# Packing the two score triangles of the C heads into one block, with the spreading on GpSimd

## The chip, the cores and the metric

The kernel runs on one NeuronCore of a Trainium2 chip. The metric is the device time of one execution in microseconds (us), the median of the runs shown. Engines are named as in the profile: PE (TensorE, matmuls; PEld its weight loads), DVE (VectorE), ACT (ScalarE), POOL or GpSimd, and SP, whose queue issues most DMAs. `L739` means line 739 of the kernel before; the changed kernel has line numbers of its own.

## The reference, cut to what matters

One layer of a hybrid decoder over 512 tokens of width 2048: RMS norm, one input projection, three token mixers side by side (A: 8 dilated heads, B: a convolution, C: 16 sliding-window heads), an output projection with residual, then a SwiGLU feed-forward with residual. All in float32. The change touches mixer C alone:

```python
def _band_attention(q, k, v, max_dist, sinks=None):
    """Causal banded attention: query t attends keys t-max_dist .. t."""
    ...
    s = jnp.einsum('nbqhgd,nbkhd->nbhgqk', qb, kb) * (hd ** -0.5)
    ...
    valid = (dist >= 0) & (dist <= max_dist) & (kpos[:, None, :] >= 0)
    s = jnp.where(valid[None, :, None, None], s, -jnp.inf)
    m = jnp.max(s, axis=-1)
    m = jnp.maximum(m, sk)                      # sk: one learned sink per head
    p = jnp.exp(s - m[..., None])
    denom = jnp.sum(p, axis=-1) + jnp.exp(sk - m)
    o = jnp.einsum('nbhgqk,nbkhd->nbqhgd', p, vb) / denom_t[..., None]
...
cq = _rms_norm(cq.reshape(B, S, C_Q_HEADS, HEAD_DIM), c_q_g[l])
ck = _rms_norm(ck.reshape(B, S, C_KV_HEADS, HEAD_DIM), c_k_g[l])
out_c, _ = _band_attention(cq, ck, cv, C_WINDOW - 1, sinks=c_sinks[l])
```

With a window of 128 and blocks of 128 queries, a query block i sees its own key block (there the lower triangle is valid, the diagonal included) and the block before (there the strict upper triangle is valid). The two triangles have no column in common: each query has at most 128 valid keys.

## The kernel before, in words

Activations lie transposed, 128 channels by 512 tokens in a tile. The program has four stages, one behind the other on PE: the input projection, tile by tile (`PROJ`, L315 to L317), the output projection (the same lines, tiles `o`), the gate and up products (L1089) and the down product (L1347 to L1349). Every float32 product is made of three fp32r matmuls: each operand is split into a high part (an ACT cast) and a low part (a DVE subtraction), and high x high, high x low and low x high are summed. The weights are split on the fly: ACT casts the high part (`wh`, L286), DVE subtracts to get the low part (`wl`, L264), two units of weights ahead of PE, with three buffers for each part.

The order is written out by hand. The mixers run in the shadow of the input projection: `project` issues 48 matmuls a tile, and at every second k step it calls `ticks.tick()`, which issues what is due at that tick on all engines (`Ticks.after(n, fn)`). Six projection matmuls lie between two ticks, and each engine runs its instructions in the order of issue. The convolution's taps (L524, L526, on DVE, one every 1.9 ticks) and its gate product (L517, on GpSimd) are placed the same way.

A C projection tile `cq` holds two heads. `head_scales` gets their RMS scales: a square on ACT, a sum on DVE, a DMA out and back, then three small GpSimd instructions (L606 to L608) that write `rq`. `attention` then places two heads, `every` = 6 ticks apart, by `C_TICKS = (ready, every, step, s1, sx, s2, fl, ev, we)`. For one C head, in ticks from its start t0:

| tick | function | what it issues |
|---|---|---|
| 0 and 2 | `scores` u = 0, 1 | PE, L739 and L740: scores of query blocks 0, 1 (u = 0; 128 + 256 keys) and 2, 3 (u = 1; 256 + 256) into a PSUM bank each |
| 2 and 4 | `top` | DVE, L746: adds the mask `bias_c` and takes the row maxima; L749 and L751 turn them into the exponent's bias |
| 4 and 6 | `exps` | ACT, L759 with the row sums; L762 for the sink |
| 6 and 8 | `norm` | DVE, L768, L773, L775: divides by the row sums |
| 13 and 14 | `flip` | PE, L791: transposes of 128x128 blocks, four and then three |
| 14 and 15 | `high` | ACT, L797: high part of the transposed block |
| 15 and 16 | `low` | DVE, L802: low part |
| 19 | `weigh` | PE, L815 and L816: eight matmuls with the values |
| 20 and 21 | `out_high`, `out_rows` | ACT L824 and DVE L829: into the tile `mix_c` |

`UNITS` lists which scores share a bank, `TBANKS` which transposed blocks stand side by side, so that one key block serves two query blocks in one matmul. Tiles of 128x512 come from one pool of `N_SLOTS` = 73 slots; a tile that is written into a slot waits for the last reader of the slot's tile before. PSUM has six banks for the mixers and two for the projection. A heads go through the same functions with `A_TICKS`, behind the C heads.

Of the kernel before, what the change touches and what calls it, by code (L numbers as in the profile page):

```python
# [24 lines left out]
BIG = -1.0e30  # L25
# [13 lines left out]
SD, VD, EV = 7, 4, 1  # L39


C_TICKS = (1, 6, 2, 2, 2, 2, 5, 1, 3)
A_TICKS = (0, 8, 2, 1, 3, 1, 3, 1, 2)


# [36 lines left out]
C_G1, C_G2, C_CW, C_CB, C_LG, C_LB, C_QK, C_SINK, C_ALL = 0, 16, 32, 156, 160, 164, 168, 172, 188  # L82
# [34 lines left out]
def kernel(ctx: ExitStack, tc: tile.TileContext, xT, wi, wo, wgu, wd, cst_in, outT):  # L117
    nc = tc.nc
# [89 lines left out]
    for t, (g, r) in enumerate(DOWN):  # L208
        first, end = RANGES[r]
        base = len(works)  # L210
# [5 lines left out]
        for k in ("21A", "11A", "21B", "11B", "22A", "22B", "12A", "12B"):  # L216
            c = k[2]
# [128 lines left out]
    ident = cp.tile([P, P], F32, name="ident")  # L346
# [4 lines left out]
    def col(i):  # L351
        return cst[:, i:i + 1]
# [17 lines left out]

    mult_a = slot("mult_a")
    bias_a = slot("bias_a")
    bias_c = slot("bias_c", cols=2 * P)
    gqk = cp.tile([P, 2], F32, name="gqk")
    nsink = cp.tile([P, 16], F32, name="nsink")
    di = slot("di", I32)
    nc.gpsimd.iota(di, pattern=[[-1, T]], base=3 * P, channel_multiplier=1)
    di2 = slot("di2", I32)
    nc.gpsimd.iota(di2[:, :2 * P], pattern=[[-1, 2 * P]], base=P, channel_multiplier=1)

    def masks():
        df, m4, r = slot("df"), slot("m4", I32), slot("r")
        nc.vector.tensor_copy(df, di)
        nc.vector.tensor_single_scalar(m4, di, 3, op=ALU.bitwise_and)
        nc.vector.tensor_scalar(r, m4, 0.0, None, op0=ALU.is_equal)
        nc.vector.scalar_tensor_tensor(mult_a, df, 128.0, r, op0=ALU.is_le, op1=ALU.add)
        nc.vector.tensor_single_scalar(m4, di, 15, op=ALU.bitwise_and)
        nc.vector.tensor_scalar(r, m4, 0.0, None, op0=ALU.is_equal)
        nc.vector.tensor_add(mult_a, mult_a, r)
        nc.vector.scalar_tensor_tensor(mult_a, df, 0.0, mult_a, op0=ALU.is_ge, op1=ALU.mult)  # L390
        nc.vector.tensor_scalar(bias_a, mult_a, 0.0, BIG, op0=ALU.is_equal, op1=ALU.mult)
        nc.vector.tensor_copy(df[:, :2 * P], di2[:, :2 * P])
        nc.vector.tensor_scalar(r[:, :2 * P], df[:, :2 * P], 127.0, None, op0=ALU.is_le)
        nc.vector.scalar_tensor_tensor(r[:, :2 * P], df[:, :2 * P], 0.0, r[:, :2 * P], op0=ALU.is_ge, op1=ALU.mult)
        nc.vector.tensor_scalar(bias_c, r[:, :2 * P], 0.0, BIG, op0=ALU.is_equal, op1=ALU.mult)
        for i in range(2):
            nc.vector.scalar_tensor_tensor(gqk[:, i:i + 1], col(C_QK + 2 * i), 8.0, col(C_QK + 2 * i + 1),
                                           op0=ALU.mult, op1=ALU.mult)
        nc.vector.tensor_scalar(nsink, cst[:, C_SINK:C_SINK + 16], -1.0, None, op0=ALU.mult)
# [42 lines left out]
    for k in range(KT):  # L442
# [9 lines left out]
        elif k < 4 or k % 2 == 0:  # L452
            wh, wl = next_unit()
            o = 0
# [9 lines left out]
        hi, lo = h_hl.pop(k)  # L464
# [15 lines left out]
    r1b = slot("r1b")  # L480
# [199 lines left out]
    def do_v(box, b, name):  # L680
# [35 lines left out]
    def attention(kind, box, mix, mi, heads):  # L716
        ready, every, step, s1, sx, s2, fl, ev, we = C_TICKS if kind == "c" else A_TICKS

        if mi in ROWS[-2:]:
            fl, we = fl + 2, we + 3  # L720
        name = mi
        us = UNITS[kind]
        mask = bias_c if kind == "c" else bias_a
        mw = mask.shape[-1]
        st = {}

        def head(h):
# [5 lines left out]
            def scores(u):  # L733
# [3 lines left out]
                for i, k0, n, o in us[u]:  # L737
                    qs, ks = slice(i * P, (i + 1) * P), slice(k0, k0 + n)
                    nc.tensor.matmul(b[:, o:o + n], q[:, qs], kh[:, ks], start=True, stop=False)  # L739
                    nc.tensor.matmul(b[:, o:o + n], q[:, qs], kl[:, ks], start=False, stop=True)  # L740

            def top(u):
                b, rq = banks[u], box["rq"]
                s = slice(us[u][0][0], us[u][-1][0] + 1)
                for i, k0, n, o in reversed(us[u]):
                    nc.vector.tensor_tensor_reduce(b[:, o:o + n], b[:, o:o + n], mask[:, mw - n:],  # L746
                                                   op0=ALU.add, op1=ALU.max, scale=1.0, scalar=-3.0e38,
                                                   accum_out=mx[:, i:i + 1])
                nc.vector.scalar_tensor_tensor(nm[:, s], mx[:, s], -1.0, rq[:, s, h], op0=ALU.mult, op1=ALU.mult)  # L749
                if kind == "c":  # L750
                    nc.vector.tensor_scalar(nm[:, s], nm[:, s], nsink[:, heads[h]:heads[h] + 1], None, op0=ALU.min)  # L751

            def exps(u):
                b, rq = banks.pop(u), box["rq"]
                e = es[u] = slot(f"{name}e{h}{u}")
                s = slice(us[u][0][0], us[u][-1][0] + 1)
                for i, k0, n, o in us[u]:
                    acc = dict(accum_out=den[:, i:i + 1]) if kind == "c" else {}
                    nc.scalar.activation(e[:, o:o + n], b[:, o:o + n], AF.Exp, bias=nm[:, i:i + 1],  # L759
                                         scale=rq[:, i, h:h + 1], **acc)  # L760
                if kind == "c":
                    nc.scalar.activation(mx[:, s], nm[:, s], AF.Exp, bias=col(C_SINK + heads[h]))  # L762

            def norm(u):
                e = es[u]
                s = slice(us[u][0][0], us[u][-1][0] + 1)
                if kind == "c":
                    nc.vector.tensor_add(den[:, s], den[:, s], mx[:, s])  # L768
                else:
                    for i, k0, n, o in us[u]:  # L770
                        nc.vector.scalar_tensor_tensor(e[:, o:o + n], e[:, o:o + n], 1.0, mult_a[:, T - n:],
                                                       op0=ALU.mult, op1=ALU.mult, accum_out=den[:, i:i + 1])
                nc.vector.reciprocal(rd[:, s], den[:, s])  # L773
                for i, k0, n, o in us[u]:
                    nc.vector.tensor_scalar(e[:, o:o + n], e[:, o:o + n], rd[:, i:i + 1], None, op0=ALU.mult)  # L775
# [244 lines left out]
        ticks.tick()  # L1020
    lows_now()
    ticks.drain()
    b = m_hi = m_lo = r1b = mult_a = bias_a = bias_c = None

    lows_now()
    late_lows.clear()
# [467 lines left out]
```

## Time and profile before

| what | value |
|---|---|
| median of 3 runs | 1872.05 us (1872.03 to 1872.28) |
| profiled execution, its own time | 1872.28 us |
| its span, first to last instruction | 1870.5 us |
| PE busy | 1864.2 us (100%) |
| DVE, ACT, POOL busy | 1466.2, 1345.4 and 1072.9 us |
| granted TensorE clock | 1.00 |
| C heads, first scores to last weigh | 99 to 331 us |

The span is what the profile covers; the run's own time holds some 1.8 us more. Busy time is the time in which an engine had an instruction under way; matmuls overlap, so a row's duration on PE is longer than the distance to the next row's start. In rows of a timeline the first number is the start, the second the duration, both in us, and a bracket at the end gives the idle time before it and what ended it.

### The profile page before, as it was taken

The numbers are of one execution on the slowest core, as the hardware profiler recorded it, in microseconds if no ns is written. First come the engines' busy times: TensorE is split into PE (matmuls) and PEld (weight loads), VectorE is DVE, ScalarE is ACT, GpSimd is POOL, SyncE is SP. The second block draws the span as 40 slices with busy tenths as digits, with TensorE's granted clock in tenths as the row PEclk, the third lists the DMA queues.
The fourth block names the chain that finished last, engine by engine and source line by source line (L and its number), as shares of the span: only waits on it lengthen the run. The fifth ranks groups of instructions, "written<-read, shape, count | busy, mean of one in ns | idle before, by whom it ended". The sixth has DMA issues, their size and how long they took to land.

```text
span 1870.5 us, 28387 instructions
## 1 busy us (share of the span) xinstructions
PE 1864.2 (100%) x9654; PEld 1597.0 (85%) x9654; DVE 1466.2 (78%) x2451; ACT 1345.4 (72%) x1872; POOL 1072.9 (57%) x700
## 2 busy tenths in 40 slices
PE   9999999999999999999999999999999999999998
PEld 7888888888888888888888888888888888888887
DVE  6789978998689777777777777777777777777767
ACT  6356654553457888888888888888888877778775
POOL 0111011100003877877878778787787879879775
PEclk9999999999999999999999999999999999999999
DMA  7242243343333445565555645556456967666645
GB/s 272 83 138 80 86 131 101 93 125 135 119 135 112 136 169 159 159 194 155 180 158 157 195 156 180 158 159 194 143 169 238 325 217 239 214 225 230 205 134 113
DMA packets 213329, 307.39 MB, mean 164 GB/s; under 512 B 75200, under 2 KB 124992, under 8 KB 213184
## 3 DMA queue, kind: packets, MB, share of 16 engines
q1 hardware_dynamic: 213040, 305.57, 51.2%
q8 instruction: 76, 1.25, 0.3%
q14 instruction: 69, 0.57, 0.1%
q10 hardware_dynamic: 144, 0.01, 0.0%
HBM read 244.03 MB, written 53.09 MB: 159 GB/s over the span
## 4 chain that ended last, share of the span: by engine, by line
PE 100%; DVE 0%; issue 0%; ACT 0%; DVEq 0%
PE out L1089 46%; PE out L1349 7%; PE out L1348 7%; PE out L1347 7%; PE o L315 3%; PE o L317 3%; PE o L316 3%; PE cq L315 2%; PE cq L317 2%; PE cq L316 2%; PE aq L317 1%; PE aq L315 1%; PE ak L315 1%; PE av L315 1%; PE ak L317 1%; PE av L316 1%
## 5 line engine op out<-in xcount | busy, mean ns | idle before, releaser
L1089 PE MATMUL out<-h,wh 128*128 128x512 f32 x2464 | 588.6, 391 | 0.0
L1089 PEld LDWEIGHTS out<-h,wh 128*128 128x128 f32 x2464 | 452.9, 188 | 87.3
L1089 PEld LDWEIGHTS out<-h,wl 128*128 128x128 f32 x2464 | 315.9, 191 | 12.0
L1089 PE MATMUL out<-h,wl 128*128 128x256 f32 x2464 | 319.7, 283 | 0.0
L1347 PE MATMUL out<-wh,a 128*128 128x512 f32 x620 | 240.6, 388 | 0.0
L1349 PE MATMUL out<-wh,a 128*128 128x512 f32 x620 | 240.5, 388 | 0.0
L1348 PE MATMUL out<-wl,a 128*128 128x512 f32 x620 | 240.5, 388 | 0.0
L286 ACT CAST wh<-w 128x1024 fp32r<-128x1024 f32 (+2 forms) x94 | 96.8, 1031 | 141.7 <-PE o L316 62.6
L264 DVE TENSOR_TENSOR wl<-w,wh 128x1024 fp32r<-128x1024 f32 (+2 forms) x95 | 112.7, 1187 | 31.3 <-ACT wh L286 31.0
L1348 PEld LDWEIGHTS out<-wl,a 128*128 128x128 f32 x620 | 116.4, 188 | 24.0
L1347 PEld LDWEIGHTS out<-wh,a 128*128 128x128 f32 x620 | 116.4, 188 | 23.8
L1349 PEld LDWEIGHTS out<-wh,a 128*128 128x128 f32 x620 | 116.4, 188 | 23.7
L1357 DVE TENSOR_TENSOR y<-y,out 128x512 f32<-128x512 f32 x164 | 106.4, 683 | 26.5 <-PE out L1349 24.9
L526 DVE SCALAR_TENSOR_TENSOR y<-bu,cst,y 128x511 f32<-128x511 f32 (+14 forms) x120 | 87.4, 729 | 0.4
L315 PE MATMUL o<-mh_c,wh 128*128 128x512 f32 x128 | 51.1, 399 | 0.0
L315 PE MATMUL cq<-hh,wh 128*128 128x512 f32 x128 | 51.1, 399 | 0.0
L317 PE MATMUL o<-mh_c,wl 128*128 128x512 f32 x128 | 50.0, 391 | 0.0
L317 PE MATMUL cq<-hh,wl 128*128 128x512 f32 x128 | 50.0, 391 | 0.0
L316 PE MATMUL o<-ml_c,wh 128*128 128x512 f32 x128 | 49.9, 390 | 0.0
L316 PE MATMUL cq<-hl,wh 128*128 128x512 f32 x128 | 49.9, 390 | 0.0
L431 POOL TENSOR_TENSOR lvr<-lvv,nhalf 128x4 f32<-128x4 f32 x1 | 1.9, 1919 | 70.8 <-DVE lvv L430 70.8
L182 POOL TENSOR_TENSOR w('s', 'g0')_5732<-w('21', 'g0')_5578,w('22', 'g0')_5576 128x1024 f32<-128x1024 f32 x1 | 2.5, 2457 | 69.0 <-DVE wl L264 69.0
(2999 smaller groups left out, 4930.9 us busy)
## 6 DMA issues: line engine op xcount, KB each, us to landing
od<-a SPq DMA_DIRECT2D x154, 256.0 KB, 4.7
a<-od SPq DMA_DIRECT2D x154, 256.0 KB, 5.6
w<-in_wi SPq DMA_DIRECT2D x58, 512.0 KB, 3.5
w<-in_wo SPq DMA_DIRECT2D x32, 512.0 KB, 3.5
x<-in_xT SPq DMA_DIRECT2D x16, 256.0 KB, 6.9
xr<-in_xT SPq DMA_DIRECT2D x16, 256.0 KB, 3.7
x2d<-xr SPq DMA_DIRECT2D x16, 256.0 KB, 2.0
z<-x2d SPq DMA_DIRECT2D x64, 64.0 KB, 3.7
```

What stands on the lines that cost most here:

```text
L182: nc.gpsimd.tensor_add(out[:, :n], raws[key[a]][0][:, :n], raws[key[b]][0][:, :n])
L264: fn(*args)
L286: (nc.vector.tensor_copy if u == 0 else nc.scalar.copy)(hi[:, :n], t[:, :n])
L315: nc.tensor.matmul(out, wh, xh, start=start, stop=False)
L316: nc.tensor.matmul(out, wh, xl, start=False, stop=False)
L317: nc.tensor.matmul(out, wl, xh, start=False, stop=stop)
L526: nc.vector.scalar_tensor_tensor(yconv[j][:, i:], hconv[j][:, :T - i], c, yconv[j][:, i:], op0=ALU.mult, op1=ALU.add)
L1089: nc.tensor.matmul(out, lhs[:, s], rhs, start=begin, stop=x is xs[-1] and low == flip[0], skip_group_check=True)
L1347: nc.tensor.matmul(b[:, lo:hi], x[:, high], wh[:, s], start=start, stop=False, skip_group_check=True)
L1348: nc.tensor.matmul(b[:, lo:hi], x[:, high], wl[:, s], start=False, stop=False, skip_group_check=True)
L1349: nc.tensor.matmul(b[:, lo:hi], x[:, low], wh[:, s], start=False, stop=last, skip_group_check=True)
L1357: getattr(eng, op)(t, t, src)
```

## The change

In a C head, `pack` takes the place of `top`. Query block 0 is masked as before (its upper triangle gets -1e30). For blocks 1, 2 and 3 a predicated copy on DVE overwrites the upper triangle of the head's own key block with the upper triangle of the block before, in PSUM, so that one block of 128x128 holds all valid scores, and the row maxima are taken over it. The four packed blocks are exponentiated on ACT in one go at tick 6, normalised on DVE by one broadcast multiply at tick 9 and transposed at tick 14 by four transposes into one bank. ACT makes the high part at tick 15, DVE the low part at tick 16. `spread_out` then writes the tiles that `weigh` reads: eight GpSimd selects (`affine_select`) a head, four on the high and four on the low part, which copy the valid triangle of each block and write zero elsewhere: six of 128x256 and two of 128x128. `weigh` is the same as before, at tick 21. The masks change to match: `bias_c` shrinks to 128 columns and a mask `upper` of 128 columns is added, both in one slot. The A heads' functions lose their branches for C.

```diff
--- before.py
+++ after.py
@@ -39,7 +39,7 @@
 SD, VD, EV = 7, 4, 1
 
 
-C_TICKS = (1, 6, 2, 2, 2, 2, 5, 1, 3)
+C_TICKS = (1, 6, 2, 2, 2, 3, 5, 1, 4)
 A_TICKS = (0, 8, 2, 1, 3, 1, 3, 1, 2)
 
 
@@ -370,13 +370,14 @@
 
-    bias_c = slot("bias_c", cols=2 * P)
+    over = slot("over")
+    bias_c, upper = over[:, :P], over[:, P:2 * P].bitcast(I32)
     di2 = slot("di2", I32)
-    nc.gpsimd.iota(di2[:, :2 * P], pattern=[[-1, 2 * P]], base=P, channel_multiplier=1)
+    nc.gpsimd.iota(di2[:, :P], pattern=[[-1, P]], base=0, channel_multiplier=1)
 
     def masks():
         df, m4, r = slot("df"), slot("m4", I32), slot("r")
@@ -389,10 +390,9 @@
         nc.vector.tensor_add(mult_a, mult_a, r)
         nc.vector.scalar_tensor_tensor(mult_a, df, 0.0, mult_a, op0=ALU.is_ge, op1=ALU.mult)
         nc.vector.tensor_scalar(bias_a, mult_a, 0.0, BIG, op0=ALU.is_equal, op1=ALU.mult)
-        nc.vector.tensor_copy(df[:, :2 * P], di2[:, :2 * P])
-        nc.vector.tensor_scalar(r[:, :2 * P], df[:, :2 * P], 127.0, None, op0=ALU.is_le)
-        nc.vector.scalar_tensor_tensor(r[:, :2 * P], df[:, :2 * P], 0.0, r[:, :2 * P], op0=ALU.is_ge, op1=ALU.mult)
-        nc.vector.tensor_scalar(bias_c, r[:, :2 * P], 0.0, BIG, op0=ALU.is_equal, op1=ALU.mult)
+        nc.vector.tensor_copy(df[:, :P], di2[:, :P])
+        nc.vector.tensor_scalar(upper, df[:, :P], 0.0, None, op0=ALU.is_lt)
+        nc.vector.tensor_scalar(bias_c, df[:, :P], 0.0, BIG, op0=ALU.is_lt, op1=ALU.mult)
         for i in range(2):
             nc.vector.scalar_tensor_tensor(gqk[:, i:i + 1], col(C_QK + 2 * i), 8.0, col(C_QK + 2 * i + 1),
                                            op0=ALU.mult, op1=ALU.mult)
...
+            def pack(u):
+                b = banks[u]
+                if u == 0:
+                    nc.vector.tensor_tensor_reduce(b[:, :P], b[:, :P], bias_c, op0=ALU.add, op1=ALU.max,
+                                                   scale=1.0, scalar=-3.0e38, accum_out=mx[:, :1])
+                    nc.vector.copy_predicated(b[:, 2 * P:3 * P], upper, b[:, P:2 * P])
+                    nc.vector.tensor_reduce(mx[:, 1:2], b[:, 2 * P:3 * P], axis=mybir.AxisListType.X, op=ALU.max)
+                else:
+                    pairs = b.rearrange("p (i a c) -> p a i c", a=2, c=P)
+                    nc.vector.copy_predicated(pairs[:, 1], upper[:, None].to_broadcast([P, 2, P]), pairs[:, 0])
+                    nc.vector.tensor_reduce(mx[:, 2:], pairs[:, 1], axis=mybir.AxisListType.X, op=ALU.max)
+                    nc.vector.scalar_tensor_tensor(nm, mx, -1.0, box["rq"][:, :, h], op0=ALU.mult, op1=ALU.mult)
+                    nc.vector.tensor_scalar(nm, nm, nsink[:, heads[h]:heads[h] + 1], None, op0=ALU.min)
+
+            def packed_exps():
+                e = es["e"] = slot(f"{name}e{h}")
+                for i in range(NT):
+                    o = (0, 2 * P, P, 3 * P)[i]
+                    nc.scalar.activation(e[:, i * P:(i + 1) * P], banks[i // 2][:, o:o + P], AF.Exp, bias=nm[:, i:i + 1],
+                                         scale=box["rq"][:, i, h:h + 1], accum_out=den[:, i:i + 1])
+                banks.clear()
+                nc.scalar.activation(mx, nm, AF.Exp, bias=col(C_SINK + heads[h]))
+
+            def packed_norm():
+                nc.vector.tensor_add(den, den, mx)
+                nc.vector.reciprocal(rd, den)
+                by = es["e"].rearrange("p (i c) -> p i c", c=P)
+                nc.vector.tensor_mul(by, by, rd[:, :, None].to_broadcast([P, NT, P]))
+
+            def packed_flip():
+                b = bank(f"{name}t{h}")
+                for i in range(NT):
+                    s = slice(i * P, (i + 1) * P)
+                    nc.tensor.transpose(b[:, s], es["e"][:, s], ident)
+                es.clear()
+                ticks.after(ev, packed_high, b)
+
+            def packed_high(b):
+                hi = slot(f"{name}hp{h}", F32R)
+                nc.scalar.copy(hi, b)
+                ticks.after(EV, packed_low, b, hi)
+
+            def packed_low(b, hi):
+                lo = slot(f"{name}lp{h}", F32R)
+                nc.vector.tensor_sub(lo, b, hi.bitcast(F32))
+                spread_out(hi, ph, "ph")
+                ticks.after(1, spread_out, lo, pl, "pl")
+
+            def spread_out(src, parts, what):
+                by = src.rearrange("p (i c) -> p i c", c=P)
+                for t in range(2):
+                    parts[t] = slot(f"{name}{what}{h}{t}", F32R)
+                    to = parts[t].rearrange("p (i c) -> p i c", c=P)
+                    nc.gpsimd.affine_select(to[:, :3:2], by[:, 2 * t:2 * t + 2], pattern=[[0, 2], [1, P]],
+                                            compare_op=ALU.is_ge, fill=0.0, base=0, channel_multiplier=-1)
+                    n = 2 - t
+                    nc.gpsimd.affine_select(to[:, 1:2 * n:2], by[:, 2 * t + 1:2 * t + 1 + n], pattern=[[0, n], [-1, P]],
+                                            compare_op=ALU.is_gt, fill=0.0, base=0, channel_multiplier=1)
+
...
             for u in range(len(us)):
                 tu = t0 + u * step
                 ticks.after(tu, scores, u)
+                if kind == "c":
+                    ticks.after(tu + s1, pack, u)
+                    continue
                 ticks.after(tu + s1, top, u)
                 ticks.after(tu + s1 + sx, exps, u)
                 ticks.after(tu + s1 + sx + s2, norm, u)
-            for t in range(len(TBANKS[kind])):
-                ticks.after(t0 + (len(us) - 1) * step + s1 + sx + s2 + fl + t, flip, t)
+            tu = t0 + (len(us) - 1) * step + s1 + sx
+            if kind == "c":
+                ticks.after(tu, packed_exps)
+                ticks.after(tu + s2, packed_norm)
+                ticks.after(tu + s2 + fl, packed_flip)
+            else:
+                for t in range(len(TBANKS[kind])):
+                    ticks.after(tu + s2 + fl + t, flip, t)
             ticks.after(t0 + at_v, weigh)
```

More of the change, by code (lines that the diff above doesn't have):

```diff
@@ L722, in attention @@
         us = UNITS[kind]
-        mask = bias_c if kind == "c" else bias_a
-        mw = mask.shape[-1]
         st = {}
@@ L745, in top @@
                 for i, k0, n, o in reversed(us[u]):
-                    nc.vector.tensor_tensor_reduce(b[:, o:o + n], b[:, o:o + n], mask[:, mw - n:],
+                    nc.vector.tensor_tensor_reduce(b[:, o:o + n], b[:, o:o + n], bias_a[:, T - n:],
                                                    op0=ALU.add, op1=ALU.max, scale=1.0, scalar=-3.0e38,
@@ L749, in top @@
                 nc.vector.scalar_tensor_tensor(nm[:, s], mx[:, s], -1.0, rq[:, s, h], op0=ALU.mult, op1=ALU.mult)
-                if kind == "c":
-                    nc.vector.tensor_scalar(nm[:, s], nm[:, s], nsink[:, heads[h]:heads[h] + 1], None, op0=ALU.min)
             def exps(u):
@@ L755, in exps @@
                 e = es[u] = slot(f"{name}e{h}{u}")
-                s = slice(us[u][0][0], us[u][-1][0] + 1)
                 for i, k0, n, o in us[u]:
-                    acc = dict(accum_out=den[:, i:i + 1]) if kind == "c" else {}
                     nc.scalar.activation(e[:, o:o + n], b[:, o:o + n], AF.Exp, bias=nm[:, i:i + 1],
-                                         scale=rq[:, i, h:h + 1], **acc)
-                if kind == "c":
-                    nc.scalar.activation(mx[:, s], nm[:, s], AF.Exp, bias=col(C_SINK + heads[h]))
+                                         scale=rq[:, i, h:h + 1])
             def norm(u):
@@ L766, in norm @@
                 s = slice(us[u][0][0], us[u][-1][0] + 1)
[L767 to L772, printed above, removed]
+                for i, k0, n, o in us[u]:
+                    nc.vector.scalar_tensor_tensor(e[:, o:o + n], e[:, o:o + n], 1.0, mult_a[:, T - n:],
+                                                   op0=ALU.mult, op1=ALU.mult, accum_out=den[:, i:i + 1])
                 nc.vector.reciprocal(rd[:, s], den[:, s])
@@ L1022 @@
     ticks.drain()
-    b = m_hi = m_lo = r1b = mult_a = bias_a = bias_c = None
+    b = m_hi = m_lo = r1b = mult_a = bias_a = bias_c = over = upper = None
     lows_now()
```

## The prediction

> **What bounds the kernel now.** I read the page's busy times and slices first, then the busy time by stretches, then the chain that ended last, and last the timeline of single heads.
>
> ```profile
> span 1870.5 us, 28387 instructions
> PE 1864.2 (100%) x9654; PEld 1597.0 (85%) x9654; DVE 1466.2 (78%) x2451; ACT 1345.4 (72%) x1872; POOL 1072.9 (57%) x700
> ...
> POOL 0111011100003877877878778787787879879775
> ```
> ```profile
> 95.00:336.00 241.00, 241.00 (x1262) 205.15 (x1261) 213.36 (x557) 142.60 (x313) 30.25 (x38) 1.00 0.37 107
> 160.00:226.50 66.50, 66.50 (x362) 57.20 (x361) 62.49 (x174) 46.48 (x104) 7.27 (x8) 1.00 0.26 80
> ```
>
> Columns of the second: stretch, sum, then PE, PEld, DVE, ACT, POOL, clock. The sixteen C heads lie between 95 and 336 us. There PE is busy in every microsecond, DVE 89% (94% where heads follow each other closest), GpSimd 13%. So time goes only if PE gets less to issue, and comes only if PE is made to wait. A busy PE is not one at its peak (the records overlap), so I price PE work by the distance between starts:
>
> ```profile
> 231.16 0.39 PE L317 MATMUL cq<-hh,wl 128*128 128x512 f32 x1
> 231.39 0.49 PE L791 MATMUL c7t<-ident,c7e 128*128 128x128 f32 x3
> 231.63 0.48 PE L315 MATMUL cq<-hh,wh 128*128 128x512 f32 x1
> 231.95 0.39 PE L316 MATMUL cq<-hl,wh 128*128 128x512 f32 x1
> ...
> 250.17 0.28 PE L816 MATMUL c7o<-c7pl,cv 128*128 128x128 f32 x1
> ...
> 250.56 0.39 PE L316 MATMUL av<-hl,wh 128*128 128x512 f32 x1
> ```
> ```profile
> 197.39 0.28 PE L816 MATMUL c5o<-c5pl,cv 128*128 128x128 f32 x1
> 197.51 0.62 PE L791 MATMUL c5t<-ident,c5e 128*128 128x128 f32 x4
> ...
> 198.20 0.39 PE L316 MATMUL bg<-hl,wh 128*128 128x512 f32 x1
> ```
>
> A projection matmul holds PE for 0.23 us (231.16 to 231.39). Three transposes between such matmuls cost 231.95 - 231.16 - 2 x 0.23 = 0.33 us. The second pair (a weigh's last matmul with no transposes behind it, up to the second matmul after it) is what the third fence has with four transposes in between. Four behind a weigh cost (198.20 - 197.39) - (250.56 - 250.17) = 0.81 - 0.39 = 0.42 us, so one is about 0.11 us.
>
> **The change, part by part.**
>
> *PE.* Seven transposes a head become four; scores and weigh keep their matmuls, so PE issues 16 x 3 = 48 fewer. In most heads four transposes stood behind a weigh and three ahead of the next scores; now four stand where the three stood: 0.42 - 0.11 = 0.31 us saved. In the first heads of c0, c3, c4 and c6 the four stood alone, and the group of three simply goes: about 0.33. Sum: 12 x 0.31 + 4 x 0.33 = 5.0 us, bounds 16 x 0.30 and 16 x 0.34 = 4.8 and 5.4. All of it is on the path, as PE waits for nothing there.
>
> *DVE.*
> ```profile
> L746 DVE CUSTOM_DVE_ANT_0 c5s<-c5s,bias_c x8: 299/424/432, 165.4 to 182.3; 128x256 f32<-128x256 f32 x6, 128x128 f32<-128x128 f32 x2
> L746 DVE DVE_READ_ACCUMULATOR2_ANT c5d<- x8: 131/141/143, 165.8 to 182.6; 128x1 f32 x8
> L751 DVE TENSOR_SCALAR c5d<-c5d,nsink x4: 228/228/229, 166.6 to 183.0; 128x2 f32<-128x2 f32 x4
> L775 DVE TENSOR_SCALAR c5e<-c5e,c5d 128x256 f32<-128x256 f32 x6 | 1.9, 350 | 0.1
> L802 DVE TENSOR_TENSOR c5pl<-c5t,c5ph 128x512 fp32r<-128x512 f32 x2 | 1.4, 684 | 0.0
> L802 DVE TENSOR_TENSOR c5pl<-c5t,c5ph 128x384 fp32r<-128x384 f32 x2 | 1.1, 552 | 0.0
> ```
> Gone per head: three masked maxima of 256 and three accumulator reads (3 x 0.43 + 3 x 0.14 = 1.71), four scalings (about 3 x 0.35 + 0.29 = 1.34), the 384-wide low (0.55), and one of each pair of four small operations (0.23 by L751's row, others less; 4 x 0.2 = 0.8): 4.4 us. (Three numbers between slashes are the shortest, median and longest in ns; behind a bar stand busy us, mean ns and idle time.) New: two predicated copies and two row maxima in PSUM, and one broadcast multiply of 512 (0.68 by the low's row). The trace has neither of the first two; bounds are half and twice the masked maximum of the same width (0.30 for 128, 0.43 for 256). I take its row, as it too reads PSUM and a mask: 4 x about 0.36 + 0.68 = 2.1. DVE loses 2.3 us a head, bounds 3.0 and 0.8. The masks lose a few small operations at the start. This is off the path.
>
> *ACT.* Four exponentials of 128 for one of 128 and three of 256, one sink exponential for two, one high for two: less in each; worth nothing, since ACT is busy 46.48 of 66.5 us there. No DMA is added or removed.
>
> *GpSimd.* Eight selects a head, six of 256 elements and two of 128, four on the highs behind ACT's copy and four on the lows behind DVE's subtraction.
> ```profile
> masks.py:199 POOL TENSOR_SCALAR_AFFINE_SELECT ident<-ident x1: 292/292/292, 1.0 to 1.0; 128x128 f32<-128x128 f32 x1
> 208.60 1.29 POOL L517 TENSOR_TENSOR bu<-bu,bg 128x512 f32<-128x512 f32 x1 [1.27 <-ACT bg L516]
> 208.79 1.52 DVE L775 TENSOR_SCALAR c2e<-c2e,c2d 128x256 f32<-128x256 f32 x2
> 344.60 1.31 POOL L606 TENSOR_TENSOR aq1r<-aq1t 128x8 f32<-128x8 f32 x1 [29.94 <-DMA aq1t<-aq1d]
> 344.59 1.21 DVE L264 TENSOR_TENSOR wl<-w,wh 128x1024 fp32r<-128x1024 f32 x1
> 95.01 0.20 POOL L606 TENSOR_TENSOR cq0r<-cq0t 128x8 f32<-128x8 f32 x1 [9.21 <-DMA cq0t<-cq0d]
> 95.57 1.64 POOL L608 TENSOR_TENSOR cq0r<-cq0r,nhalf 128x8 f32<-128x8 f32 x1
> ```
> ```profile
> L264 DVE TENSOR_TENSOR wl<-w,wh 128x1024 fp32r<-128x1024 f32 x9 | 11.0, 1218 | 1.5 <-ACT wh L286 1.5
> L526 DVE SCALAR_TENSOR_TENSOR y<-bu,cst,y 128x511 f32<-128x511 f32 (+14 forms) x120 | 87.4, 729 | 0.4
> ```
> One of 128 took 0.29. Twice that bounds one of 256 from above if no start-up is shared; 0.4 is the other end (0.29 plus 128 elements at half the multiply's 1.29 us for 512, halved again for one input). I take 0.55: 6 x 0.55 + 2 x 0.29 = 3.9 us a head (bounds 3.0 and 4.1), alone. They are not alone. GpSimd's tiny L606 takes 0.20 us, but 1.31 where DVE's L264 started with it and ended with it; DVE's two scalings take 0.7 together, but 1.52 while GpSimd multiplied. So each engine can hold up the other by one instruction. The Trainium skill (SBUF — State Buffer, section Who interferes with whom) says that a DVE instruction with two SBUF inputs contends with a GpSimd one that reads SBUF, and that the loser fully blocks; both pairs of rows agree with it. L264 reads two tensors from SBUF, and of DVE's work only the taps do so as often: 9 of L264 in the 66.5 us of 160 to 226.5 are 1.8 us in a head's 10.8 us (next paragraph), and the taps (0.73 us each, one every 1.9 ticks, 3.2 a head) 2.3 us. So a select meets one 4 times in 10 and then waits for about half of it, up to 0.6 us: 0.25 us more on the mean, 0.75 a select, some 5.9 us a head. The other way round, five such DVE instructions meet a select 4 times in 10 and wait about 0.3 us: 0.6 us a head, less than the 2.3 that DVE loses.
>
> *Who waits now.* Weigh waits for GpSimd; behind it on PE stands everything.
> ```profile
> 186.67 0.62 PE L791 MATMUL c5t<-ident,c5e 128*128 128x128 f32 x4
> 187.48 0.59 ACT L797 CAST c5ph<-c5t 128x512 fp32r<-128x512 f32 x1
> 188.52 0.49 PE L791 MATMUL c5t<-ident,c5e 128*128 128x128 f32 x3
> 189.97 0.69 DVE L802 TENSOR_TENSOR c5pl<-c5t,c5ph 128x512 fp32r<-128x512 f32 x1
> 192.60 0.55 DVE L802 TENSOR_TENSOR c5pl<-c5t,c5ph 128x384 fp32r<-128x384 f32 x1
> 196.62 0.28 PE L815 MATMUL c5o<-c5ph,cv 128*128 128x256 f32 x1
> ```
> The flip moves to tick 14 (now 188.52 for this head) and weigh to tick 21, seven ticks later. Heads of six ticks lie 197.51 - 186.67 = 10.84 us apart, so seven are 12.6, less 0.3 saved: 12.3 us. High ends 1.4 us and low 4.0 us after the flip's start here (4.6 for the second pair, which began at 192.60). The high selects (2.9 us) start at 1.4 and end at 4.3; the low ones end at 4.6 + 2.9 = 7.5, in a late head, I allow, at 9. Three to five microseconds are left, and these hide the selects. In GpSimd's order the head scales (L606 to L608, 0.2 + 0.2 + 1.64 us) and the gate multiply (L517, 1.29) stand between selects of some heads, head scales even between the highs and the lows of one c5 head; that takes 2 to 3 us of the margin, not all. Who waits behind them on GpSimd: rq, which the next head's maxima need a projection later, and the taps of bu2 and bu3; both are wanted some ticks later.
>
> *Slots.* A head takes seven, not six, of the 73 rotating slots, so late in the stage writers wait for readers sooner.
> ```profile
> 278.85 0.69 DVE L632 TENSOR_TENSOR cq6l<-cq6raw,cq 128x512 fp32r<-128x512 f32 x1 [1.91 <-PE c4o L816]
> 280.13 0.54 SPq L637 DMA_DIRECT2D cq<-cq6l  x1
> 286.65 0.22 PE L739 MATMUL c6s<-ckh,cq 128*128 128x128 f32 x1
> 339.20 0.42 DVE L802 TENSOR_TENSOR a0pl<-a0t,a0ph 128x256 fp32r<-128x256 f32 x1
> 339.68 0.39 PE L816 MATMUL a0o<-a0pl,av 128*128 128x256 f32 x1
> ```
> Here DVE already waits for a weigh; afterwards it waits for the low selects of the same head, and SP's twin copies and the c6 scores follow. Those scores start at 286.65, 6 us after the copies' issue ended, so I cost this at nothing, and at the excess if the selects are later than that. The tightest place of all is head a0: its last low ends at 339.62 and PE uses it at 339.68. In the changed order c6's addition into the mix (64x512, about 0.7) stands behind that low and no longer ahead of it, while a0's lows come behind aq1's low, which now waits for c6's later weigh: some 0.7 earlier, some 0.3 later. Nothing, at worst one DVE instruction, 0.7 us.
>
> *Sum.* 1870.5 - 5.0 = 1865.5 us of span; the profiled run's own time is 1.78 us above its span, and the median shown 0.23 below that run: 1867.0.
>
> **Rivals.**
>
> *GpSimd sets the pace (slower).* Eight selects have to fit into a head's 10.5 us. Above 1.3 us a select they don't, and each further head is later at weigh; the first 4 us of that are margin, the next 5 eat the saving. Over the twelve heads that follow closely the sign turns where 12 x (8s - 10.5) = 9, at s = 1.4 us. With the full wait that L606 shows on every select (0.55 + 1.1 = 1.65 us) it is 12 x 2.7 - 4 = 28 us: 1895. For it: DVE is busy 94%, so a two-input instruction is nearly always near, and a strided fp32r select isn't in the trace. Against: the wait is for the rest of one instruction, and DVE gets emptier. The Trainium skill's rule above makes such waits sure and leaves their number open.
>
> *Single late heads (no change).* Only where head scales or a slot fall between does weigh wait, 1 us in three or four heads: 1870 to 1871. For it: head scales in the middle of c5; against: the margin of 3 us.
>
> *The transposes don't count (no change).* If four transposes ahead of scores cost what seven did apart, 1872. The rows of three and four speak against it.
>
> **How the numbers follow.** A measurement can tell 0.2%, 3.7 us, from no change. Forecast, 1866.2 to 1868.3, its own range: 0.66. Single late heads, up to 1875.8: 0.11; no saving: 0.03. GpSimd's pace, above 1875.8: 0.18. More saved: 0.02. The range has to reach into the slower case: 1865.5 to 1885, leaving out about 0.12.
>
> **What would show it.** Right: PE with 48 fewer matmuls, busy in the whole of 95 to 331, no wait of PE for GpSimd; selects of 256 at 0.5 to 0.9 us; DVE in the stage below 89%. Wrong: idle PE ahead of weigh, released by a select; selects above 1.2 us; L264 or the taps stretched, and weights' lows late.

## The result, and the profile after

The changed kernel takes 1867.24 us (median of 9 runs, 1866.96 to 1869.81), the kernel before 1872.28 beside it (1872.03 to 1872.55): a ratio of 0.9975, with a 95% interval of 0.9965 to 0.9985. That is 5.0 us less; 1867.0 was forecast.

From the page of the changed kernel, its span, its busy times and GpSimd's slices; then its busy time by stretches (stretch, sum, then PE, PEld, DVE, ACT, POOL, each with its count, clock, DMA share, GB/s):

```profile
span 1865.9 us, 28280 instructions
PE 1858.8 (100%) x9606; PEld 1591.2 (85%) x9606; DVE 1446.7 (78%) x2290; ACT 1330.5 (71%) x1840; POOL 1141.7 (61%) x828
...
POOL 0125533100013877888878878788787878779775
```
```profile
95.00:331.00 236.00, 236.00 (x1213) 200.42 (x1212) 194.97 (x397) 127.46 (x281) 99.41 (x166) 1.00 0.39 110
160.00:221.50 61.50, 61.50 (x331) 52.79 (x330) 53.43 (x107) 40.18 (x91) 34.37 (x54) 1.00 0.29 86
```

PE has 48 matmuls fewer and is still busy in every microsecond of the stage, now 95 to 331. DVE fell from 89% to 83% there (194.97 of 236), in the dense part (six heads that follow each other closest, the second row) from 94% to 87%; GpSimd rose from 13% to 42%, in the dense part to 56%.

Where the time went is read from one matmul in both traces. The projections are the same 2196 matmuls in the same order; these are number 384 (counted from 0), near the start of the stage, and number 1248, behind its end, first before and then after:

```profile
97.42 0.39 PE L315 MATMUL cq<-hh,wh 128*128 128x512 f32 x1
345.39 0.39 PE L315 MATMUL aq<-hh,wh 128*128 128x512 f32 x1
```
```profile
97.75 0.39 PE L315 MATMUL cq<-hh,wh 128*128 128x512 f32 x1
340.51 0.39 PE L315 MATMUL aq<-hh,wh 128*128 128x512 f32 x1
```

Between them lie 247.97 and 242.76 us: 5.21 us saved, or 0.108 for each of the 48 transposes. Up to the first one this execution was 0.33 later (PE waited 0.41 us for its first weights), and what follows the second took 0.28 longer, so the spans differ by 4.6.

Two heads show the room that weigh has for GpSimd. First the first head of c5, from its last transposes (185.53) to weigh, with the selects' rows on POOL:

```profile
185.53 0.60 PE L773 MATMUL c5t<-ident,c5e 128*128 128x128 f32 x4
186.88 0.77 POOL L793 TENSOR_SCALAR_AFFINE_SELECT c5ph<-c5hp 128x256 fp32r<-128x256 f32 x1 [1.56 <-ACT c5hp L779]
187.96 0.40 POOL L793 TENSOR_SCALAR_AFFINE_SELECT c5ph<-c5hp 128x256 fp32r<-128x256 f32 x1
191.50 0.29 POOL L796 TENSOR_SCALAR_AFFINE_SELECT c5pl<-c5lp 128x128 fp32r<-128x128 f32 x1
198.33 0.28 PE L863 MATMUL c5o<-c5ph,cv 128*128 128x256 f32 x1
```

The last select ends at 191.79 and weigh starts at 198.33: 6.5 us of room. The second head of c0 has next to none:

```profile
134.18 0.83 POOL L606 TENSOR_TENSOR cq1r<-cq1t 128x8 f32<-128x8 f32 x1 [6.17 <-DMA cq1t<-cq1d]
135.37 2.09 POOL L608 TENSOR_TENSOR cq1r<-cq1r,nhalf 128x8 f32<-128x8 f32 x1
137.42 0.41 POOL L793 TENSOR_SCALAR_AFFINE_SELECT c0ph<-c0hp 128x256 fp32r<-128x256 f32 x1
140.76 1.27 POOL L796 TENSOR_SCALAR_AFFINE_SELECT c0pl<-c0lp 128x128 fp32r<-128x128 f32 x1
142.07 0.28 PE L863 MATMUL c0o<-c0ph,cv 128*128 128x256 f32 x1
```

There GpSimd waits 6.2 us for the DMA of cq1's norm sums, with the selects of a head that is long flipped behind it, and the last select, itself stretched from 0.29 to 1.27, ends at 142.03, 0.04 us ahead of weigh. In the other fifteen heads the room is 1.7 to 6.5 us, and PE waits for GpSimd nowhere.

### The profile page after: what moved, and what is told of

Same layout as the page of the kernel before. It is cut to its first block, busy times and chain, and to the rows that moved or that the text cites. A ratio compares the mean times of both kernels' runs of the same rounds, so it can differ in the third digit from the quotient of the medians.

```text
span 1865.9 us, 28280 instructions
## 1 busy us (share of the span) xinstructions
PE 1858.8 (100%) x9606; PEld 1591.2 (85%) x9606; DVE 1446.7 (78%) x2290; ACT 1330.5 (71%) x1840; POOL 1141.7 (61%) x828
## 4 chain that ended last, share of the span: by engine, by line
PE 99%; DMA 0%; SPq 0%; DVE 0%; issue 0%; ACT 0%; DVEq 0%
PE out L1146 46%; PE out L1405 7%; PE out L1404 7%; PE out L1406 7%; PE o L317 3%; PE o L315 3%; PE o L316 3%; PE cq L315 2%; PE cq L317 2%; PE cq L316 2%; PE ak L315 1%; PE aq L315 1%; PE av L315 1%; PE aq L317 1%; PE aq L316 1%; PE av L316 1%
## 5 line engine op out<-in xcount | busy, mean ns | idle before, releaser
L264 DVE TENSOR_TENSOR wl<-w,wh 128x1024 fp32r<-128x1024 f32 (+2 forms) x95 | 113.2, 1191 | 41.1 <-ACT wh L286 39.5
```

The source lines that it names most:

```text
L264: fn(*args)
```

## The experiments

Theory one, as predicted: the saving is the PE time of 48 transposes, and all the rest is hidden. Its main rivals were that another part of the change saves the time, and that GpSimd is close to setting it. A second theory came out of the first run. Times stand beside the kernel before on the same chip (1872.57, 1872.78 or 1872.58); a ratio's interval is about ±0.001, 1.9 us, so smaller differences are read from traces.

### The transposes alone

In the kernel before, the second group of transposes goes, and nothing else:

```diff
             def flip(t):
-                b = bank(f"{name}t{h}{t}")
+                again = kind == "c" and t == 1
+                b = banks["t"] if again else bank(f"{name}t{h}{t}")
+                banks["t"] = b
...
-                        nc.tensor.transpose(b[:, o:o + P], block(i, j), ident)
+                        if not again:
+                            nc.tensor.transpose(b[:, o:o + P], block(i, j), ident)
```

> The kernel before, without the second group of three transposes of every C head (48 fewer; the second group's high and low are taken from the first group's bank instead, so that the attention output is wrong and everything else stays in its place). Theory one, the saving is the PE time of 48 transposes and the rest of the change is hidden: 1872.3 less 48 x 0.108 (5.2 us between the first projection of the stage and the last in the two traces) = 1867.1, PE never waiting. Rival, the saving comes from the emptier DVE and ACT or from shorter chains, and the transposes don't count: within 0.5 of 1872.3. Between the two: both have a share.

It took 1871.88 us (11 runs, 1870.45 to 1873.13), a ratio of 0.9996 (0.9987 to 1.0005): almost nothing was saved. That is the number of the rival, so only the trace tells what happened; it shows the fastest of these runs, 1870.45. The one wait of PE in the stage, and the rows of the chain that ended it (the scales of the key ak2, from its squares on ACT to PE):

```profile
PE ak2t L655 <- ACT ak2wide L648: 3.2, 1, 3.2
```
```profile
218.53 0.64 ACT L582 ACTIVATE ak2sq<-ak2raw 128x512 f32<-128x512 f32 x1
224.73 0.71 DVE L587 TRANSPOSE_TENSOR_REDUCE ak2p<-ak2sq 128x16 f32<-128x512 f32 x1
232.59 1.22 DVE L264 TENSOR_TENSOR wl<-w,wh 128x1024 fp32r<-128x1024 f32 x1
232.74 1.12 POOL L606 TENSOR_TENSOR ak2r<-ak2t 128x8 f32<-128x8 f32 x1 [21.91 <-DVE c7pl L805]
233.94 0.55 POOL L607 TENSOR_TENSOR ak2r<-ak2r,c 128x8 f32<-128x8 f32 x1
236.25 0.62 ACT L648 COPY ak2wide<-ak2r 128x512 f32<-128x512 f32 x1 [5.00 <-POOL ak2r L608]
236.92 0.33 PE L655 MATMUL ak2t<-ident,ak2wide 128*128 128x128 f32 x1 [3.16 <-ACT ak2wide L648]
```

The same chain in the kernel before, and in the changed one:

```profile
221.14 0.63 ACT L582 ACTIVATE ak2sq<-ak2raw 128x512 f32<-128x512 f32 x1
225.22 0.71 DVE L587 TRANSPOSE_TENSOR_REDUCE ak2p<-ak2sq 128x16 f32<-128x512 f32 x1
235.10 0.62 ACT L648 COPY ak2wide<-ak2r 128x512 f32<-128x512 f32 x1 [0.27 <-POOL ak2r L608]
237.21 0.60 PE L655 MATMUL ak2t<-ident,ak2wide 128*128 128x128 f32 x4
```
```profile
217.36 0.63 ACT L582 ACTIVATE ak2sq<-ak2raw 128x512 f32<-128x512 f32 x1
221.91 0.71 DVE L587 TRANSPOSE_TENSOR_REDUCE ak2p<-ak2sq 128x16 f32<-128x512 f32 x1
231.89 0.62 ACT L648 COPY ak2wide<-ak2r 128x512 f32<-128x512 f32 x1 [0.52 <-POOL ak2r L608]
234.03 0.49 PE L655 MATMUL ak2t<-ident,ak2wide 128*128 128x128 f32 x3
```

With fewer transposes the squares of ak2 are ready 2.6 us earlier than before (219.17 against 221.77), but DVE takes them only 0.5 earlier: it has its full load still and doesn't get ahead with PE. In the changed kernel it takes them 3.3 us earlier, and ACT ends 1.5 us ahead of PE (232.51 against 234.03), as it did before (235.72 against 237.21). So theory two: the transposes give 5.2 us (without its wait this run's stage is 5.2 us shorter too: the two projections lie 245.91 us apart, 3.16 of it the wait), but only a DVE with less to do lets PE keep them.

Not all of the 3.16 us is that lateness. From the end of L587 to the start of ak2wide the chain took 10.8 us here and 9.2 before; 1.3 of this came on GpSimd, where L606 and L607 took 1.12 and 0.55 instead of 0.20 each while DVE ran a weight's low (L264) and a tap beside them. And the median run is 1.4 us slower than the traced one; where it lost that isn't shown.

### The transposes and the scalings

As above, and the four scalings of a head by its softmax denominator left out:

```diff
-                for i, k0, n, o in us[u]:
+                for i, k0, n, o in us[u] if kind == "a" else []:
                     nc.vector.tensor_scalar(e[:, o:o + n], e[:, o:o + n], rd[:, i:i + 1], None, op0=ALU.mult)
```

> The run less_before (48 fewer transposes in the kernel before), and also without the four scalings by the softmax denominator of every C head on DVE (about 1.5 us a head; the attention isn't normalised). In less_before PE saved 5.3 us in the stage and then stood still for 3.2 us ahead of the transposes of ak2's scales: DVE reached the reduction of ak2's squares (L587) at 224.73, 5.6 us after they were ready, and DMA, GpSimd, ACT and PE followed. Theory two, DVE's backlog sets that wait, so the removal of transposes pays only together with less work for DVE: the wait goes and the time is 1867.0 (1866.3 to 1868). Rival, the wait comes from the DMAs or from GpSimd's order in that place, not from DVE's load: it stays, 1871.9.

1867.66 us, ratio 0.9973 (0.9963 to 0.9983): the whole gain, without GpSimd in it. The wait at ak2 is gone from the trace (DVE takes the squares at 221.45, 3.3 us earlier than with the scalings), and PE waits nowhere in the stage. Theory two holds: it is DVE's work that set the wait. How much of it by DVE's lateness and how much by holding GpSimd up, this run doesn't tell apart.

### DVE's work put back

In the changed kernel, in `pack`:

```diff
-                    nc.vector.tensor_reduce(mx[:, 2:], pairs[:, 1], axis=mybir.AxisListType.X, op=ALU.max)
+                    for again in range(5):
+                        nc.vector.tensor_reduce(mx[:, 2:], pairs[:, 1], axis=mybir.AxisListType.X, op=ALU.max)
```

> The changed kernel, with the last row maximum of each C head's pack (256 wide, in PSUM, 0.42 us) taken five times instead of once: 1.7 us more for DVE in a head, 27 us in all, which is about what the change took from it (241.1 to 212.3 us of DVE instructions in the stage). Output unchanged, PE has as little to do as in the changed kernel. Theory two: DVE lags again, PE waits at the scales of ak2 or another key for 2 to 5 us, 1869 to 1872. Theory one (only PE's own work counts): 1867.2.

1879.28 us, ratio 1.0036 (1.0023 to 1.0048): the gain is gone, and 6.5 us more. This is above both expectations. The traced run is the slowest of the five, at 1881.25 (the others 1879.0 to 1879.4). The largest waits of PE in its trace:

```profile
PE c2o L865 <- POOL c2pl L797: 2.3, 2, 2.0
PE c2s L737 <- DVE c1lp L785: 1.7, 1, 1.7
PE ckt L655 <- ACT ckwide L648: 1.6, 1, 1.6
PE c5o L865 <- POOL c5pl L797: 1.5, 1, 1.5
```

The wait at ckt ends at 89.8, ahead of the first C head, so the added work didn't make it; it is the traced run's own. I had looked for the wait at a key's scales. Of the 7.5 us of waiting in the stage 5.1 came at weigh instead: a late DVE makes the low part late, GpSimd's four selects come behind that, and weigh behind them. The chain is longer by an engine than before, and with about as much DVE work as before PE now waits (248.4 us of DVE instructions between the two projections of above, 249.5 before). The five maxima stand in a row at the head of a C head's chain, though, and how much their place costs besides their amount these runs don't tell. The same edit with `range(3)`, half the extra work:

> The run busy_dve with half the extra work: the last row maximum three times instead of once, 0.85 us a head more for DVE, 13.5 us in all. If DVE's lateness grows only once it has more work than time (in busy_dve PE began to wait in earnest at 189 us, where heads follow each other in 10.5 us): DVE is at 53.4 of 61.5 us there, 0.85 more a head makes 95%, so nearly nothing yet, 1867.2 to 1869. If the cost is in proportion to the work: half of 12, 1873.

1868.61 us, ratio 0.9979 (0.9970 to 0.9988), with 1.9 us of waiting at c5's and c0's weigh in the trace. Measured against the kernel before on the same chip, half the work takes some 1.1 us off the gain and all of it 11.5, so the cost isn't proportional. DVE is busy 93% of the dense part with half (56.95 of 61.5 us) and 96% with all (63.74 of 66.5): the cost begins where DVE is nearly full.

### The spread on DVE

```diff
-                    nc.gpsimd.affine_select(to[:, :3:2], by[:, 2 * t:2 * t + 2], pattern=[[0, 2], [1, P]], ...)
+                    nc.vector.tensor_mul(to[:, :3:2], by[:, 2 * t:2 * t + 2].bitcast(F32),
+                                         own[:, None].to_broadcast([P, 2, P]))
...
```

> The changed kernel with the spread on DVE instead of GpSimd: each select becomes a multiplication by a 0/1 triangle (two more 128x128 masks, same values). Eight of them are 6 x 0.37 + 2 x 0.2 = 2.6 us a head more for DVE, from the broadcast multiplication of 512 at 0.69. Theory two, DVE's load is the second bound: 1.7 us a head more (busy_dve) cost 12 us; 2.6 less the 0.25 that the selects hold DVE up, without the wait for GpSimd behind it, 1885 (1876 to 1895), DVE at 95% of the stage or more. Rival, DVE in its order ahead of weigh has room, as the chain gets shorter by one engine: 1867 to 1870.

1882.64 us, ratio 1.0053 (1.0040 to 1.0067). Busy time by stretches, and the largest waits of PE:

```profile
160.00:226.50 66.50, 62.81 (x326) 52.42 (x325) 64.68 (x152) 38.74 (x90) 11.08 (x8) 0.99 0.25 76
```
```profile
PE ak2t L658 <- ACT ak2wide L651: 4.0, 1, 4.0
PE c2o L866 <- DVE mix_c L880: 1.5, 1, 1.5
```

DVE is busy 97% of the dense part (64.68 of 66.5; 90% of the whole stage, where 95% was expected) and PE no longer all of it: DVE has become the bound, and the largest wait is the one at ak2 again. That the spread lies on GpSimd is what the gain depends on.

### The transposes put back

```diff
-                for i in range(NT):
+                for i in (0, 1, 2, 3, 0, 1, 2):
                     s = slice(i * P, (i + 1) * P)
                     nc.tensor.transpose(b[:, s], es["e"][:, s], ident)
```

> The changed kernel, with the first three of the four transposes of each C head issued a second time to the same place (48 more, so as many matmuls as before; the output is unchanged). Theory one: all the saving goes, 1867.2 + 5.2 = 1872.4. Rival, the transposes don't count: 1867.2 to 1868.

1872.41 us, ratio 0.9999 (0.9990 to 1.0008): the price of a transpose is confirmed from the other side, by an emptier DVE that brings nothing once PE has its work back.

### Weigh earlier and later

`C_TICKS` ends in 3, in 2 and in 5 instead of 4.

> The changed kernel with weigh one tick earlier (C_TICKS ends in 3 instead of 4). Theory one, the selects end 1.7 to 6.5 us ahead of weigh in all heads but the second of c0 (0.04 us): only that head's weigh waits for GpSimd, for 1.8 us less the 0.6 us by which the last select is used after the first matmul of weigh, about 1.1 us, so 1868.4 (1867.2 to 1869.2). Rival, the selects have far more room than the trace says and nothing waits: 1867.2. Rival, GpSimd is already at its pace and each head's wait adds up: 16 x 1 us, above 1875.

> The changed kernel with weigh two ticks earlier. Theory one, by the room of each head in the trace (3.6 us less room less 0.6, where positive): c0's second 3.0, c4's second 1.3, c7's second 0.9, c1's and c2's second 0.5 each, c5's second 0.1: 6.3 us of waiting, 1873.5 (1870 to 1877), PE waiting for GpSimd in five or six heads. Rival, more room than the trace says: below 1869. Rival, waits add up over all heads: above 1880.

> The changed kernel with weigh one tick later (C_TICKS ends in 5): 1.8 us more room for the selects of every head, c0's second among them. Theory one: PE has as little to do as before and there is no wait left to remove in most executions, 1866.9 to 1867.3, with no execution above 1868.5. Rival, slots come free later and the last C heads or a0's lows make PE wait: 1868 to 1870.

One tick earlier: 1867.30 us, ratio 0.9972 (0.9961 to 0.9983); two of its seven runs lie at 1868.92 and 1869.31. The traced run is the latter, and its one new wait stands where it was expected. Two ticks earlier: 1871.65 us, ratio 0.9996 (0.9987 to 1.0005). One tick later: 1867.57 us, ratio 0.9974 (0.9963 to 0.9984), with one run at 1868.52, both a little above what was expected (1867.3, and no run above 1868.5). The waits of PE in the stage one tick earlier, then two:

```profile
PE c0o L864 <- POOL c0pl L796: 2.0, 2, 1.0
```
```profile
PE c4o L864 <- POOL c4pl L796: 0.7, 1, 0.7
PE c2o L864 <- POOL c2pl L796: 0.6, 1, 0.6
PE c7o L864 <- POOL c7pl L796: 0.3, 1, 0.3
```

The second list is short of the loss, some 4 us, because the profile counts as idle only what goes beyond the end of the record before. The first two matmuls of weigh in c4's second head, two ticks earlier:

```profile
286.69 0.28 PE L863 MATMUL c4o<-c4ph,cv 128*128 128x256 f32 x1
287.65 0.39 PE L864 MATMUL c4o<-c4pl,cv 128*128 128x256 f32 x1 [0.69 <-POOL c4pl L796]
```

They start 0.96 us apart, 0.12 in the changed kernel, and the bracket has 0.69 of it. From the first start to the last, weigh's eight matmuls take 0.77 or 0.78 us in all sixteen heads of the changed kernel, and more in seven heads here, 3.5 us in all: 1.07, 0.87 and 0.74 in the second heads of c4, c2 and c7, and 0.1 to 0.3 in four others.

The heads that wait longest are among those that had the least room by the trace. c0's second head waits in some executions only: its selects stand behind a head scale that waits for a DMA, and in the trace of two ticks earlier that scale began at 133.20 instead of 134.56 (the trace of one tick earlier) and the head lost 0.1 us. Tick 21 is late enough, a later one brings nothing, and two earlier lose nearly all.

### The selects twice, and not at all

```diff
                 for t in range(2):
...
+                    for again in range(2):
...
```

> The changed kernel with every select issued twice in a row (same output): GpSimd has 16 selects a head, 8.6 us at the measured mean of 0.54, in heads of about 10.3 us. Theory one, the room of each head counts: the low selects end about 4.3 us later and the room was 1.7 to 6.5 us, and 0.04 in c0's second; about nine heads wait, by 12 us in all at most and by some 9 if they wait as little as weigh2 showed (4.4 where 6.3 was worked out): 1876 (1871 to 1882). Rival, GpSimd's pace as the prediction had it, from 1.3 us a select on: with head scales and gates it has about 10.9 us of work a head, 0.6 us too much in each of twelve heads on top of the margin: about 1884. Rival, GpSimd is far from the path: 1867.2.

1873.53 us, ratio 1.0001 (0.9992 to 1.0010). Busy time by stretches of the dense part and of a place at 145 us, and the waits of PE:

```profile
160.00:226.50 66.50, 66.50 (x356) 57.09 (x356) 59.41 (x119) 40.77 (x92) 57.86 (x111) 1.00 0.30 88
145.00:148.00 3.00, 3.00 (x9) 2.52 (x10) 0.69 (x1) 0.58 (x1) 1.80 (x3) 0.51 0.09 26
```
```profile
PE c0o L865 <- POOL c0pl L797: 2.3, 2, 1.5
PE c7o L865 <- POOL c7pl L797: 1.7, 2, 1.3
```

Three heads wait (c0's second, c7's first, and c4's first by 0.3), not nine. In six heads 0.2 to 3.0 us still lie between the last high select and the first low one, so that doubling the high ones moves nothing there and only the low ones count. Room alone doesn't name the heads: c7's first had 3.2 us of it and c4's first 3.4, and heads with less didn't wait. The two that lose most have a head scale in front of their selects (L608, 133.37 to 136.06 and 234.98 to 237.49). With GpSimd busy 87% of the dense part (57.86 of 66.5) the trace shows no wait of PE there. So GpSimd's pace is not the bound even at twice the selects; what is lost is lost in single heads.

Without the selects (weigh takes the packed tiles):

> The changed kernel without its 128 selects: weigh takes the packed high and low as they are (so the attention is wrong), and GpSimd has nothing new to do. Theory one, the selects are hidden but for rare waits in c0's second head: 1866.8 to 1867.3, and no execution above 1868.5 (the changed kernel had one of nine at 1869.81). Rival, the selects hold DVE or PE up by a little everywhere: below 1866.3.

1867.05 us, ratio 0.9971 (0.9961 to 0.9982), one of seven runs at 1868.44. The times don't tell it from the changed kernel, and in its trace the two projections of above lie 242.76 us apart, as they do there. The selects cost nothing that can be measured.

### What holds a select up

```diff
-        else:
+        elif i > 99:
             nc.vector.scalar_tensor_tensor(yconv[j][:, i:], hconv[j][:, :T - i], c, yconv[j][:, i:],
```

> The changed kernel without the taps L526 of the causal convolution (they read two SBUF tensors on DVE; the conv branch then holds its first tap alone). In the changed kernel 51 of the 128 selects are longer than their shortest form (0.40 us for 256 wide, 0.29 for 128), 26.6 us in all; 21 of these have a tap alone beside them (8.7 us), 21 a tap and another such instruction (12.6), 9 another alone (5.0). Theory, a DVE instruction with two SBUF inputs holds a GpSimd select up until its end: 15 to 30 selects stretched, 8 to 14 us in all, each with L264, L632, L767 or the like beside it. Rival, the selects are stretched by DMA or other SBUF traffic: about 50 stretched, 25 us. Time: 1867 in both, as PE waits for neither (the taps come early enough for the later layer norm).

1867.28 us in one run. 22 selects are stretched, by 13.8 us in all, and each has L264, L632, L767, L670, L764, L819 or L823 beside it: the first expectation, but for L823, a scaling that reads one tensor and a column, which held one select up from 0.40 to 0.59. How it looks in the changed kernel, POOL and DVE rows of two places:

```profile
181.87 0.94 DVE L526 SCALAR_TENSOR_TENSOR y<-bu,cst,y 128x500 f32<-128x500 f32 x1
182.24 2.04 POOL L796 TENSOR_SCALAR_AFFINE_SELECT c1pl<-c1lp 128x256 fp32r<-128x256 f32 x1
182.74 1.21 DVE L264 TENSOR_TENSOR wl<-w,wh 128x1024 fp32r<-128x1024 f32 x1
...
190.95 0.69 DVE L877 TENSOR_TENSOR mix_c<-mix_c,c1o 64x512 f32<-64x512 f32 x1
191.14 0.40 POOL L793 TENSOR_SCALAR_AFFINE_SELECT c5pl<-c5lp 128x256 fp32r<-128x256 f32 x1
```

A tap and a weight's low, both with two SBUF inputs, hold one select up from 0.40 to 2.04 us. The addition into the mix reads PSUM for its second input, and the select beside it takes its 0.40. This is the rule of the Trainium skill (SBUF — State Buffer, section Who interferes with whom) that the prediction named, and both places and 21 of the 22 selects of the run agree with it; the one beside L823 suggests that a tensor and a column can be enough.

## Why the prediction was right, and where not

- **PE.** 48 transposes by some 0.105 us, 5.0 us (4.8 to 5.4): measured 5.21 in the stage. The price is confirmed in both directions: less_before's stage is 5.2 us shorter without its wait (the expectation of less_both has 5.3), and more3_after lost it all.
- **"All of it is on the path, as PE waits for nothing there."** This step was incomplete. It is true of the changed kernel, but PE waited for nothing before because it was slow enough for DVE. In less_before's trace 3.16 of those 5 us were lost again, to DVE's lateness and to GpSimd held up by DVE, and more in its median run.
- **DVE.** It was to lose 2.3 us a head, less 0.6 for being held up: 1.7. Its instructions in the stage sum to 241.1 us before and 212.3 after, which is 1.8 a head, holds included. (The copies and maxima in PSUM, which the trace before didn't have, came to 1.43 us a head; 1.44 was taken.) "This is off the path" is the sentence that fell: the relief is a condition of the gain. The total had no error by it, because the change brings both; in this step that was luck, as nothing in the sum asked for DVE's relief.
- **GpSimd alone.** I took 0.55 for a select of 256 and 0.29 for one of 128; alone they take 0.40, the lower of the two ends, and 0.29. With holds I had 0.75 on the mean; it is 0.54 (GpSimd's busy time in the stage rose by 69.2 us for 128 of them), with 51 of 128 held, 4 in 10, as worked out, for 0.52 us on the mean and up to 1.6, where 0.6 was to be the most. Of the two pairs of rows that were to agree with the rule, the second (DVE's scalings, L775) reads one tensor and a column, like L823, so it is not a plain case of two inputs.
- **The margin.** "Three to five microseconds are left": 1.7 to 6.5 in fifteen heads, 0.04 in one. That one is the mechanism of the rival of single late heads, a head scale in front of selects; it didn't cost time in the traced run. It may be behind the one run at 1869.81, but that run has no trace, and runs without any select have single slow ones too (less_both 1868.98, 1.3 us above its median; the kernel before 1874.61, 1.8 above).
- **The slower rival**, GpSimd's pace from 1.4 us a select on, was far off at 0.54. Its arithmetic stands: 16 selects of 0.55 did fit. What the rivals lacked is DVE's pace. Had the change not emptied DVE, it would by these runs have ended at no change (less_before), or slower, if DVE's load had stayed as it was behind the longer chain (busy_dve).
- **Slots.** Costed at nothing; PE waits for none.

## What to carry to other kernels

An engine that is busy all the time hides how near the next one is: before pricing work taken off it, take the same time off the margins of every engine that feeds it (here DVE, 94% busy in the dense part, and behind it a key's scales that were ready only 1.5 us ahead of PE). Work moved from one full engine to an idle third one pays through both, and adds a link to the chain: give the consumer ticks enough for it, and look in the third engine's queue for what waits for a DMA in front of the moved work.

## What the runs showed of the hardware that was not expected

A short wait of PE can cost more than itself. In double_sel PE stood still for 0.84 and 1.48 us within c0's weigh (140 to 145), and from 145 to 148 the granted clock was 0.51 (the row above): projections came 0.43 us apart instead of 0.23. In less_before one gap of 3.16 us was followed by the full clock:

```profile
237.00:240.00 3.00, 3.00 (x21) 2.75 (x22) 2.57 (x5) 2.69 (x5) 0.00 (x0) 1.00 0.06 2
```

The Trainium skill (TensorE: Matmul & The Clock Gate, section What's actually happening) says that the clock falls to half after at least one idle window of about 3.4 us, the windows running freely. Here two shorter gaps with matmuls between them were followed by the half clock once, and a longer one was not another time; what decides between them these runs don't show.
